# Where a PSUM bank, a lag and sixteen weight tiles go in a two-layer decoder kernel

## The chip, the cores and the metric

The kernel runs on one core of one Trainium2 chip. Its time is the device time of one execution in microseconds (us), median of several runs. TensorE (PE) multiplies matrices from SBUF into PSUM, which has eight banks of 128 x 512 f32 values; VectorE (DVE) and ScalarE (ACT) read PSUM and SBUF; GpSimd (POOL) works on SBUF; SyncE (SP) issues most of the loads.

## The reference

A sequence of 512 tokens of width 1024 goes through two layers. Layer A computes 12 heads of sparse attention in 3 groups of 4 (compressed blocks, selected blocks, sliding window) beside 4 heads of attention to a memory of 256 tokens, then a squared-ReLU MLP with 4096 hidden units. Layer B computes dilated attention with 3 groups of 8 heads over keys and values that are made once from the stream, again with memory attention, and a second MLP. All in float32:

```
for layer in range(2):
    h = rmsnorm(x, attn_norm[layer])
    mem_kv = rmsnorm(mem, mem_norm[layer]) @ w_mem_kv[layer]
    if layer == 0:
        q, kc, vc, ks, vs, kw, vw, q_mem, gl = split(h @ a_w_in)
        o_main = nsa_attention(q, kc, vc, ks, vs, kw, vw, gl, ...)
        w_out = a_w_out
    else:
        k_s, v_s = split(rmsnorm(x, kv_norm) @ w_kv_shared)
        k_shared = rope(rmsnorm(split_heads(k_s, 8), kv_k_norm), pos)
        q, q_mem = split(h @ b_w_in)
        o_main = dilated_attention(q, k_shared, split_heads(v_s, 8), b_q_norm)
        w_out = b_w_out
    o_mem = memory_attention(q_mem, mem_kv, mem_q_norm[layer], mem_k_norm[layer])
    x = x + concat([o_main, o_mem]) @ w_out
    x = x + square(relu(rmsnorm(x, mlp_norm[layer]) @ w_up[layer])) @ w_down[layer]
```

## The kernel before, in words

**Matmuls in three parts.** Float32 operands are split into a rounded high part and a low part, and `mm3` (lines 260 to 262) multiplies high by high, high by low and low by high into one bank. A weight tile is loaded into a staging buffer `st` (three of them) by SP, ScalarE writes its high part (`wsplit`, line 253), and VectorE or GpSimd its low part (line 255): a letter "v" or "g" says which. The string "gv" takes turns. The staging buffer is free when both parts are written, and there are four buffers `w` for the result.

**PSUM.** The eight banks lie in four pools: `pacc` (2) for projections, `pS` (2) for attention scores, `pT` (3) for transposes, `pO` (1) for attention outputs. `ps()` hands out one bank of a pool.

**Attention as items.** An `Item` has a front (scores on PE into `pS`, row maximum on VectorE at lines 1043, 1055 or 713, exponentials on ScalarE at line 216 through `marked`, scaling on GpSimd at line 722) and a back (transposes of the probabilities on PE into `pT`, copies out at line 730 by ScalarE or, in layer A every third time, VectorE, and products with the values into `pO`). `attend` runs the fronts in order and each back a number of items later (`lag`, here 1). After each front and each back, `tick` takes one step from a list `side` and, by a ratio for each segment, steps from a queue of other work `work`: the next group's projection, memory keys, the first part of the output projection. In layer A an item's scores take one bank for the first two query blocks and two for the other two; in layer B one. Layer A's scores are at lines 972 (compressed blocks), 1039 and 1052, its transposes at 996, 1081 and 1087; layer B's scores at 1536, 1540, 1544 and 1550, its transposes at 1584 and 1593.

**Projections.** `proj` multiplies in blocks of 128 tokens, each in one bank, and `evac` reads the bank: `normf` (lines 501 to 515) finds the norms of the heads by a square, a sum and a few small operations, a product with the gain follows, then rotation on GpSimd, and some steps later transposes of the result (`q_out`, lines 755 and 765) into `pT`. The first projection keeps four banks at once, two of them from `pS`. The projection `w_a0` after it takes its four banks as `pS`, `pacc`, `pacc`, `pS`, with low parts on GpSimd.

**Output projections.** `outpart` goes over eight output tiles; it is called twice in each layer, and takes its weights' low parts in turns by GpSimd and VectorE. Its first part is `work` beside the last attention items, its second comes after them. Line 1149 adds the result to the stream.

The build's scheduler orders each engine's instructions ahead of time, by the order of the program and its own model of when things are ready.

Of the kernel before, what the change touches and what calls it, by code (L numbers as in the profile page):

```python
# [11 lines left out]
ALU = mybir.AluOpType  # L12
# [7 lines left out]
HD = 64  # L20
# [13 lines left out]
def bcast(ap, dim, n):  # L34

    a = [list(x) for x in ap.ap]
    a.insert(dim, [0, n])
    return bass.AP(tensor=ap.tensor, offset=ap.offset, ap=a)
# [9 lines left out]
RB = (1.58, 1.85, 1.49, 2.4, 1.9)  # L48
# [20 lines left out]
def drain(*gens):  # L69
    for g in gens:  # L70
        for _ in g:
            pass
# [20 lines left out]
class Work:  # L93


    def __init__(self):
        self.q, self.done = [], set()
# [83 lines left out]
class K:  # L181
    def __init__(self, ctx, tc, ins, out):
        self.tc, self.nc, self.ins, self.out = tc, tc.nc, ins, out
        ps = lambda n, b: ctx.enter_context(tc.tile_pool(name=n, bufs=b, space=bass.MemoryType.PSUM))
        sb = lambda n, b: ctx.enter_context(tc.tile_pool(name=n, bufs=b))
        self.pacc, self.pS, self.pT, self.pO = ps("acc", 2), ps("ps", 2), ps("pt", 3), ps("po", 1)
        self.one = sb("one", 1)
        self.sb = sb("sb", 1)
        self.dram = ctx.enter_context(tc.tile_pool(name="dram", bufs=1, space=bass.MemoryType.DRAM))
        self.n = 0  # L190
        self.ev = 3
        self.staged = []
        self.sums, self.marks = {}, []
        self.adds, self.far = self.blocks(), 5
        self.lab = "s"
# [9 lines left out]

    def ps(self, pool, shape, dt=F32):
        self.n += 1
        return pool.tile(shape, dt, name=f"{self.lab}_{pool.name}_{self.n}", tag=pool.name)

    def c(self, name, shape, dt=F32):  # L210
        return self.one.tile(shape, dt, name=name)
# [288 lines left out]
    def normf(self, raw, nh, e):  # L500

        nc = self.nc
        p = raw.shape[0]
        sq = self.t("sq", [p, nh, HD])
        nc.scalar.activation(sq.rearrange("p h d -> p (h d)"), raw, AF.Square)
        ss = self.t("r4", [p, nh])
        nc.vector.tensor_reduce(out=ss, in_=sq, axis=AX.X, op=ALU.add)
        y = self.t("r5", [p, 3, nh])
        nc.scalar.activation(y[:, 0], ss, AF.Ln, scale=1.0 / HD, bias=e[:, 0:1])
        nc.scalar.activation(y[:, 1], y[:, 0], AF.Exp, scale=-0.5, bias=self.eps[0:p, 2:3])  # L510
        nc.scalar.activation(y[:, 2], y[:, 1], AF.Square)
        f = self.t("r6", [p, nh])
        nc.vector.scalar_tensor_tensor(out=f, in0=ss, scalar=e[:, 1:2], in1=y[:, 2], op0=ALU.add, op1=ALU.mult)
        nc.vector.scalar_tensor_tensor(out=f, in0=f, scalar=-1.5, in1=y[:, 1], op0=ALU.add, op1=ALU.mult)
        return f
# [96 lines left out]
    def mem_q(self, l, xg, wsrc, e, res):  # L612
        nc = self.nc
        q4 = [self.t("qk", [P, 2, S], F32R) for _ in range(2)]
        gq = self.grow(f"mq{l}")

        def evac(b, ps):
            f = self.normf(ps, 4, e[:, b])
            G = self.t("tq", [P, 4, HD])
            nc.vector.tensor_tensor(  # L620
                out=G, in0=ps.rearrange("p (h d) -> p h d", d=HD), in1=bcast(gq[:, 0], 1, 4), op=ALU.mult
            )
            blk = slice(b * P, (b + 1) * P)
            return self.q_out(G, f, [q4[0][:, :, blk], q4[1][:, :, blk]])

        yield from self.proj(xg, wsrc, 256, evac, per=4, lo="gv")
        res.append(q4)

    def mem_keys(self, l, kf, res):
# [485 lines left out]
    def outpart(self, oT, k0, k1, wsrc, xsrc, w0, wide=1):  # L1115


        nc = self.nc
        nk = k1 - k0
        while len(oT) < k1:  # L1120
            yield WAIT
        oT = oT[k0:k1]
        for m0 in range(0, KT, wide):
            ms = range(m0, min(m0 + wide, KT))
            w, ps = {}, {}

            def step(m, k):
                self.mm3(
                    ps[m], [w[m][:, h, k * P : (k + 1) * P] for h in (0, 1)], [oT[k][:, h, :] for h in (0, 1)],
                    k == 0, k == nk - 1,  # L1130
                )

            for m in ms:
                c = slice(w0 * P, (w0 + nk) * P)
                w[m] = self.wload(wsrc[m][:, c], "gv"[m % 2])
                ps[m] = self.ps(self.pacc if xsrc is not None else self.pS, [P, S])
                for k in range(nk - 1):
                    step(m, k)
                    yield
            for m in ms:  # L1140
                step(m, nk - 1)
                yield
                if xsrc is not None:
                    xo = self.t("st", [P, S])
                    nc.sync.dma_start(xo, xsrc[m])
                    self.x[m] = self.t("x", [P, S])
                else:
                    xo = self.x[m]
                nc.vector.tensor_tensor(out=self.x[m], in0=ps[m], in1=xo, op=ALU.add)
# [243 lines left out]
    def layer_b(self):  # L1393
        self.ev = 1000000
        nc, ins = self.nc, self.ins
        self.setup_b()
        st = self.rt
        xk = self.xk
        xd = self.xd
        vd = self.dram.tile([S, 512], F32, name="vd")  # L1400

        def evac_v(b, ps):
            t = self.t("raw", [P, 512])
            nc.scalar.activation(t, ps, AF.Copy, scale=st[0][:, b : b + 1])
            nc.gpsimd.dma_start(vd[b * P : (b + 1) * P, :], t)

        kn = [None] * NB

        gk = self.grow("kk")

        def evac_k(b, ps):
            e = st[1]
            kt = self.t("x", [P, 8, HD])
            kn[b] = kt
            for hf in range(2):
                rw = ps[:, hf * 256 : (hf + 1) * 256]
                f = self.normf(rw, 4, e[:, b])
                kh = kt[:, hf * 4 : hf * 4 + 4]
                nc.vector.tensor_tensor(
                    out=kh, in0=rw.rearrange("p (h d) -> p h d", d=HD), in1=bcast(gk[:, 0], 1, 4), op=ALU.mult  # L1420
                )
                self.rope(kh, self.cs[:, b])
                nc.gpsimd.tensor_tensor(out=kh, in0=kh, in1=bcast(f, 2, HD), op=ALU.mult)

        drain(
            self.proj(xk, ins["w_kv"][0], 512, evac_k, pool=[self.pS, self.pS, self.pacc, self.pacc], order=(2, 3, 0, 1))
        )
        drain(self.proj(xk, ins["w_kv"][1], 512, evac_v, pool=self.pS))
        xg = [self.t("act", [P, 2, S], F32R) for _ in range(KT)]
        for m in range(KT):  # L1430
            for h in range(2):
                self.gained(xg[m], m, h, "attn1")
        e = st[1]
        oT, om, pb, qm, kk = [], [], [[] for _ in range(4)], [], []
        kp, vals = [[] for _ in range(4)], [[] for _ in range(4)]
        work, side, seen = Work(), Work(), []
        for sp in range(1, 4):
            work.add(self.proj_b(sp, xg, e, pb[sp]))
            work.add(self.keys_b(sp, kn, vd, kp[sp]), sp, lambda sp=sp: seen.count(sp - 1) == 8)
        work.add(self.mem_q(1, xg, ins["w_bm"], e, qm))  # L1440
        work.add(self.mem_keys(1, self.kf1, kk), "mem")
        work.add(self.outpart(oT, 0, 3, ins["w_bo"], xd, 0))
        first = weave(self.proj_b(0, xg, e, pb[0], self.pS, DX), self.keys_b(0, kn, vd, kp[0]), WK)
        for i, _ in enumerate(first):
            for _ in range(WB[1] if i >= WB[0] else 0):
                work.step()
        items = []
        for sp in range(4):
            items += self.attn_b(sp, pb[sp], kp[sp], oT, side)
        items += self.mem_items(self.kf1, qm, kk, om, 4, "mem")  # L1450
        attend(items, work, side, RB, seen)
        while side.step() is not END or work.step() is not END:
            pass
        drain(self.outpart(oT + om, 3, 6, ins["w_bo"], None, 3, 3))
# [233 lines left out]
def build(tc, ins, out):  # L1688
    with ExitStack() as ctx:
        k = K(ctx, tc, ins, out)  # L1690
        nc = tc.nc
        k.setup()
        k.layer_a()
        k.mlp(0)
        k.layer_b()
        k.mlp(1)
# [111 lines left out]
```

## Time and profile before

| | us |
|---|---|
| median of 3 runs | 1285.7 |
| lowest and highest | 1283.59, 1286.21 |
| profiled execution, own time | 1285.64 |
| its span, first to last instruction | 1283.9 |
| PE busy | 1243.8 |
| VectorE busy | 829.8 |
| ScalarE busy | 756.1 |
| GpSimd busy | 365.7 |

The stages, in us from the start of the span: layer A's projections and attention 0 to about 335, its MLP to about 690, shared keys and values and layer B's first queries to about 790, layer B's attention to about 907, the end of its memory attention and output projection to about 937, the second MLP to the end. Matmuls overlap in PE, so that busy time is not the same as full rate; the idle time before an instruction, in brackets in the timelines, is time in which PE had nothing in flight. The granted clock is 1.00 at full speed.

### The profile page before, as it was taken

The page shows a single profiled execution, that of the slowest core. Times are in us where ns is not written, and L with a number is a line of the kernel's source. Part 1 is how long each engine was busy: PE and PEld are TensorE (multiplying, and loading weights), DVE is VectorE, ACT ScalarE, POOL GpSimd, SP SyncE. Part 2 cuts the span into 40 slices and gives each one's busy share as a digit, 9 for nine tenths or more (in the row PEclk, how much of TensorE's full clock was granted, in tenths as well). Part 3 has the DMA queues.
Part 4 walks back from the last instruction along what each step waited for, and adds up shares of the span by engine and source line. Part 5 has one row for each costly group of instructions (what it writes and reads, how often), then busy time and mean ns, then how long its engine had stood idle before and what let it go on. Part 6 is the DMA issues. An engine that isn't in the chain of part 4 may idle for free.

```text
span 1283.9 us, 18311 instructions
## 1 busy us (share of the span) xinstructions
PE 1243.8 (97%) x6416; PEld 1024.4 (80%) x6416; DVE 829.8 (65%) x1510; ACT 756.1 (59%) x1684; POOL 365.7 (28%) x470
## 2 busy tenths in 40 slices
PE   8899998899999999999999999999999999999998
PEld 6868877677788888888888899887778888888887
DVE  6746875654565657566579577676757656656566
ACT  6745777774575364453648467778657455354462
POOL 4445774543140000000002778363413000000000
PEclk9899999999999999999999999999999999999999
DMA  7521332334478797797975422110359789697434
GB/s 262 196 91 54 97 100 91 67 75 116 147 240 235 244 267 218 263 239 225 275 210 185 133 85 66 52 46 10 102 167 278 211 275 251 198 295 228 143 105 164
DMA packets 61836, 215.27 MB, mean 168 GB/s; under 512 B 6736, under 2 KB 14928, under 8 KB 61232
## 3 DMA queue, kind: packets, MB, share of 16 engines
q1 hardware_dynamic: 50800, 143.72, 34.0%
q0 software_dynamic: 9344, 35.77, 14.2%
q10 hardware_dynamic: 1600, 34.61, 7.5%
q8 instruction: 51, 0.84, 0.3%
q14 instruction: 41, 0.34, 0.1%
HBM read 208.83 MB, written 72.35 MB: 219 GB/s over the span
## 4 chain that ended last, share of the span: by engine, by line
PE 78%; DVE 8%; ACT 6%; DMA 4%; issue 2%; POOL 1%; SPq 0%; ACTq 0%; POOLq 0%; DVEq 0%
PE s_ps L260 13%; PE s_ps L261 13%; PE s_ps L262 13%; PE s_acc L260 6%; PE s_acc L261 5%; PE s_acc L262 5%; PE s_pt L260 3%; PE s_pt L261 3%; PE s_pt L262 3%; PE s_po L734 3%; ACT s_p L216 2%; DVE s_w L255 1%; PE s_ps L1052 1%; DMA s_st<-in_w_ao_dram 1%; DVE s_act L277 1%
## 5 line engine op out<-in xcount | busy, mean ns | idle before, releaser
L255 DVE TENSOR_TENSOR s_w<-s_st,s_w 128x1024 fp32r<-128x1024 f32 (+3 forms) x236 | 279.0, 1187 | 253.3 <-ACT s_w L253 252.6
L253 ACT ACTIVATE s_w<-s_st 128x1024 fp32r<-128x1024 f32 (+4 forms) x260 | 251.3, 970 | 191.1 <-DMA s_st<-sum 40.0
L260 PE MATMUL s_ps<-s_act,s_w 128*128 128x512 f32 x568 | 222.8, 394 | 2.0 <-ACT s_act L295 1.4
L261 PE MATMUL s_ps<-s_act,s_w 128*128 128x512 f32 x568 | 221.5, 391 | 0.0
L262 PE MATMUL s_ps<-s_act,s_w 128*128 128x512 f32 x568 | 221.2, 390 | 0.0
L260 PEld LDWEIGHTS s_ps<-s_act,s_w 128*128 128x128 f32 x568 | 106.4, 188 | 26.3 <-ACT s_act L295 3.2
L262 PEld LDWEIGHTS s_ps<-s_act,s_w 128*128 128x128 f32 x568 | 106.7, 188 | 22.4
L261 PEld LDWEIGHTS s_ps<-s_act,s_w 128*128 128x128 f32 x568 | 106.7, 188 | 22.2 <-DVE s_act L298 0.9
L216 ACT ACTIVATE s_p<-s_ps 128x512 f32<-128x512 f32 x64 | 38.3, 598 | 121.6 <-PE s_ps L262 120.7
L260 PE MATMUL s_acc<-s_w,s_act 128*128 128x512 f32 (+3 forms) x288 | 102.5, 362 | 4.9 <-DVE s_r L497 3.4
L261 PE MATMUL s_acc<-s_w,s_act 128*128 128x512 f32 (+3 forms) x288 | 102.6, 357 | 1.6 <-POOL s_w L255 1.5
L262 PE MATMUL s_acc<-s_w,s_act 128*128 128x512 f32 (+3 forms) x288 | 100.8, 355 | 0.0
L1170 POOL DMA_DIRECT2D sum<-in_w_db_dram x16 | 14.4, 899 | 288.8 <-ACT s_p L216 287.1
L216 ACT ACTIVATE s_p<-s_ps,s_nm 128x256 f32<-128x256 f32 (+3 forms) x128 | 65.0, 515 | 22.3 <-DVE s_nm L1055 10.2
L722 POOL TENSOR_SCALAR s_p<-s_p,s_cr,s_ab 128x128 f32<-128x128 f32 (+3 forms) x96 | 59.0, 638 | 47.5 <-DVE s_cr L1063 45.9
L260 PEld LDWEIGHTS s_acc<-s_w,s_act 128*128 128x128 f32 x288 | 55.0, 192 | 10.6 <-ACT s_x L942 3.4
L730 ACT ACTIVATE s_pt<-s_pt 128x512 f32<-128x512 f32 (+2 forms) x101 | 51.9, 523 | 15.9 <-PE s_pt L1087 5.3
L261 PEld LDWEIGHTS s_acc<-s_w,s_act 128*128 128x128 f32 x288 | 55.2, 192 | 6.4 <-POOL s_w L255 1.7
L295 ACT ACTIVATE s_qk<-s_p 128x256 fp32r<-128x256 f32 (+1 forms) x96 | 46.9, 488 | 21.0 <-DVE s_p L1180 19.1
L262 PEld LDWEIGHTS s_acc<-s_w,s_act 128*128 128x128 f32 x288 | 55.2, 192 | 4.2 <-issue 0.2
L1170 POOL DMA_DIRECT2D sum<-sum x16 | 14.1, 883 | 151.3 <-DMA sum<-sum 64.6
L298 DVE TENSOR_TENSOR s_qk<-s_p,s_qk 128x256 fp32r<-128x256 f32 (+1 forms) x96 | 50.1, 522 | 0.7 <-ACT s_qk L295 0.6
(329 smaller groups left out, 2913.9 us busy)
## 6 DMA issues: line engine op xcount, KB each, us to landing
s_st<-in_w_up_dram SPq DMA_DIRECT2D x64, 512.0 KB, 4.2
s_st<-sum SPq DMA_DIRECT2D x64, 512.0 KB, 7.3
s_st<-in_w_db_dram SPq DMA_DIRECT2D x48, 512.0 KB, 4.6
sum<-in_w_db_dram POOLq DMA_DIRECT2D x16, 1024.0 KB, 14.4
sum<-sum POOLq DMA_DIRECT2D x16, 1024.0 KB, 12.1
s_st<-in_w_bq_dram SPq DMA_DIRECT2D x16, 384.0 KB, 3.4
s_st<-in_w_ag_dram SPq DMA_DIRECT2D x11, 512.0 KB, 3.6
s_w<-in_w_c_dram SPq DMA_DIRECT2D x8, 512.0 KB, 4.5
```

The lines of the kernel that those rows point to most:

```text
L216: return lambda *a, **k: self.marks.append(f(*a, **k))
L253: nc.scalar.activation(w[:, 0], st, AF.Copy)
L255: e.tensor_tensor(out=w[:, 1], in0=st, in1=w[:, 0], op=ALU.subtract)
L260: mm(ps, lh[0], rh[0], start=start, stop=False, skip_group_check=again)
L261: mm(ps, lh[0], rh[1], start=False, stop=False, skip_group_check=again)
L262: mm(ps, lh[1], rh[0], start=False, stop=stop, skip_group_check=again)
L295: nc.scalar.activation(dst[:, 0], src, AF.Copy)
L298: nc.vector.tensor_tensor(out=dst[:, 1], in0=src, in1=dst[:, 0], op=ALU.subtract)
L722: self.nc.gpsimd.tensor_scalar(out=p, in0=p, scalar1=c, scalar2=g, op0=ALU.mult, op1=ALU.mult)
L730: self.turned = self.nc.scalar.activation(dst, src, AF.Copy)
L734: i = self.nc.tensor.matmul(*a, **k)
L1170: self.behind(self.nc.gpsimd.dma_start(t[o], x, accum_op=ALU.add, max_dma_last_dim=4096))
```

## The change

Five edits. (1) The third transpose bank becomes a pool `px` of its own, and `ps()` gives every third request of one chosen pool to it: of `pS` through layer A, of `pT` from the first MLP on. So layer A has three score banks and two transpose banks, and the rest two and three. (2) `attend` in layer B runs with a lag of 2. (3) `outpart` and `mem_q` (both layers) take the low parts of all their weights on VectorE. (4) The shared keys' norms are found over 8 heads of a block at once, and the product with the gain is one instruction; rotation and scaling stay in halves of 4 heads. (5) `normf` puts its squares into the buffers `p2` (six) where there are over 6 heads, and in `sq` (one) otherwise.

```diff
-        self.pacc, self.pS, self.pT, self.pO = ps("acc", 2), ps("ps", 2), ps("pt", 3), ps("po", 1)
+        self.pacc, self.pS, self.pT, self.pO = ps("acc", 2), ps("ps", 2), ps("pt", 2), ps("po", 1)
+        self.px, self.third, self.turns = ps("px", 1), self.pS, 0
...
     def ps(self, pool, shape, dt=F32):
         self.n += 1
-        return pool.tile(shape, dt, name=f"{self.lab}_{pool.name}_{self.n}", tag=pool.name)
+        name = f"{self.lab}_{pool.name}_{self.n}"
+        if pool is self.third:
+            self.turns += 1
+            if self.turns % 3 == 0:
+                pool = self.px
+        return pool.tile(shape, dt, name=name, tag=pool.name)
+
+    def third_to(self, pool):
+
+        self.third, self.turns = pool, 0
...
-        sq = self.t("sq", [p, nh, HD])
+        sq = self.t("p2" if nh > 6 else "sq", [p, nh, HD])
...
-        yield from self.proj(xg, wsrc, 256, evac, per=4, lo="gv")
+        yield from self.proj(xg, wsrc, 256, evac, per=4, lo="v")
...
-                w[m] = self.wload(wsrc[m][:, c], "gv"[m % 2])
+                w[m] = self.wload(wsrc[m][:, c], "v")
...
+            f = self.normf(ps, 8, e[:, b])
+            nc.vector.tensor_tensor(
+                out=kt, in0=ps.rearrange("p (h d) -> p h d", d=HD), in1=bcast(gk[:, 0], 1, 8), op=ALU.mult
+            )
             for hf in range(2):
-                rw = ps[:, hf * 256 : (hf + 1) * 256]
-                f = self.normf(rw, 4, e[:, b])
                 kh = kt[:, hf * 4 : hf * 4 + 4]
-                nc.vector.tensor_tensor(
-                    out=kh, in0=rw.rearrange("p (h d) -> p h d", d=HD), in1=bcast(gk[:, 0], 1, 4), op=ALU.mult
-                )
                 self.rope(kh, self.cs[:, b])
-                nc.gpsimd.tensor_tensor(out=kh, in0=kh, in1=bcast(f, 2, HD), op=ALU.mult)
+                nc.gpsimd.tensor_tensor(out=kh, in0=kh, in1=bcast(f[:, hf * 4 : hf * 4 + 4], 2, HD), op=ALU.mult)
...
-        attend(items, work, side, RB, seen)
+        attend(items, work, side, RB, seen, 2)
...
         k.layer_a()
+        k.third_to(k.pT)
         k.mlp(0)
```

## The prediction

> **What bounds the kernel now.** I read the busy line first, then a table by stage, then what TensorE (PE) waits for in the two attention stages, then single places in order of time. From the page, and from the table of windows (columns: stage, its length, then busy us and count for PE, weight loads, VectorE, ScalarE, GpSimd, then granted clock, DMA share, GB/s):
>
> ```profile
> PE 1243.8 (97%) x6416; PEld 1024.4 (80%) x6416; DVE 829.8 (65%) x1510; ACT 756.1 (59%) x1684; POOL 365.7 (28%) x470
> 0.00:335.00 335.00, 312.63 (x1792) 245.42 (x1792) 207.29 (x498) 213.35 (x608) 169.82 (x249) 0.97 0.37 115
> 335.00:690.00 355.00, 354.92 (x1596) 294.08 (x1597) 229.95 (x336) 194.84 (x297) 28.26 (x26) 1.00 0.81 239
> 690.00:790.00 100.00, 95.76 (x517) 86.25 (x515) 73.09 (x144) 61.85 (x173) 73.38 (x90) 0.98 0.33 103
> 790.00:907.00 117.00, 109.30 (x841) 95.64 (x840) 81.61 (x180) 89.29 (x296) 54.97 (x63) 1.00 0.14 41
> 907.00:937.00 30.00, 28.39 (x148) 19.55 (x147) 20.50 (x47) 19.26 (x56) 15.16 (x22) 1.00 0.33 100
> 937.00:1284.00 347.00, 342.85 (x1531) 283.46 (x1529) 217.36 (x311) 177.51 (x259) 24.09 (x21) 1.00 0.71 213
> ```
>
> PE is the bound: of a span of 1283.9 us it is busy 1243.8. The MLP of layer A (335 to 690) leaves 0.08 us idle, and that of layer B gives up 4 us of which the change touches nothing; so 702 us are out of reach, either way: there the third transpose bank is the same rotation of three under another name. What can move is idle time of layer A (22.4 us), of layer B's projections (4.2), its attention (7.7) and its end (1.6), 36 us together, and time at a lower clock. The waits of PE in those stages, layer A from 40 us on, then layer B:
>
> ```profile
> PE s_ps L1052 <- ACT s_p L216: 6.0, 11, 1.2
> PE s_ps L1039 <- ACT s_p L216: 3.9, 8, 1.4
> ...
> PE s_pt L1087 <- POOL s_p L722: 1.6, 3, 0.7
> PE s_pt L1081 <- ACT s_pt L730: 0.6, 1, 0.6
> ...
> PE s_pt L1584 <- ACT s_p L216: 3.5, 5, 1.4
> PE s_acc L261 <- POOL s_w L255: 1.5, 1, 1.5
> ```
>
> In layer A the scores (L1039, L1052) wait 9.9 us for exponentials, that is for one of two score banks to be read out, while the transposes wait 0.6 us for a transpose bank (s_pt released by the copy L730). In layer B the transposes (L1584) wait for exponentials.
>
> **The change part by part.** I sum against the profiled execution's own 1285.64 us; the median of the runs is 1285.7, so nothing is lost between them. The build fixes each engine's order in advance, and the order after the change is not in this trace: every term has a wide interval for that.
>
> *The bank, first use: the end of the first projection.* Four banks hold group 0's projection; the next projection (420 columns) asks for a bank of the score pool first and, having none, waits until the first is read out. With a third bank it starts at once. PE and GpSimd in order of time:
>
> ```profile
> 29.05 0.98 PE L489 MATMUL s_pt<-on,s_p 128*128 128x1 f32 x8
> 33.41 0.51 PE L260 MATMUL s_acc<-s_w,s_act 128*128 128x420 f32 x1 [3.39 <-DVE s_r L497]
> 34.07 0.55 PE L262 MATMUL s_acc<-s_w,s_act 128*128 128x420 f32 x1
> 34.42 0.55 PE L260 MATMUL s_acc<-s_w,s_act 128*128 128x420 f32 x1
> 38.10 0.35 PE L261 MATMUL s_acc<-s_w,s_act 128*128 128x420 f32 x1
> 38.29 0.35 PE L262 MATMUL s_acc<-s_w,s_act 128*128 128x420 f32 x1
> ...
> 28.88 1.96 POOL L255 TENSOR_TENSOR s_w<-s_st,s_w 128x840 fp32r<-128x840 f32 x1
> 33.54 2.17 POOL L255 TENSOR_TENSOR s_w<-s_st,s_w 128x840 fp32r<-128x840 f32 x1 [2.71 <-ACT s_w L253]
> ```
>
> PE stands 3.39 us, then issues at 0.35 us a matmul in place of 0.19 for about ten matmuls, 1.6 us more: 5.0 in all. The third weight slab is complete at 30.84 (28.88 + 1.96), so 18 matmuls of the first block could run from 30.0 to 33.4; the fourth is complete only at 35.71. If PE's order then waits for it, only about 2.7 us come back (18 matmuls done at 35.71, where now (35.71 - 33.41)/0.35 = 6.6 are done: 11.4 x 0.19 = 2.2, and 0.5 of slow clock); if the next block is drawn ahead, 5.0. I take 3.5; ends 0 and 5.0.
>
> *The bank in layer A's attention.* It is ScalarE that reads the score banks, and where PE waits longest it has little to spare. Here is a window before and one after the clock fell, three times, and two windows in layer B:
>
> ```profile
> 57.50:60.90 3.40, 1.95 (x11) 1.23 (x9) 2.67 (x7) 3.30 (x13) 0.68 (x2) 1.00 1.01 400
> 60.90:67.70 6.80, 6.10 (x23) 5.06 (x22) 4.35 (x10) 5.84 (x18) 6.80 (x17) 0.50 0.38 154
> 207.70:211.10 3.40, 2.08 (x11) 1.10 (x9) 2.57 (x8) 3.37 (x11) 1.80 (x4) 1.00 0.02 5
> 211.10:214.50 3.40, 3.27 (x18) 2.14 (x20) 1.08 (x4) 1.74 (x9) 2.70 (x6) 0.50 0.94 292
> 241.80:245.20 3.40, 1.75 (x8) 1.13 (x8) 2.54 (x9) 3.11 (x12) 0.92 (x2) 1.00 0.00 0
> 245.20:248.60 3.40, 3.03 (x10) 2.64 (x11) 2.33 (x9) 1.87 (x7) 3.22 (x7) 0.51 0.00 0
> 842.58:846.00 3.42, 1.88 (x15) 1.73 (x15) 3.42 (x4) 2.27 (x7) 3.42 (x3) 1.00 0.45 116
> 883.53:886.94 3.41, 2.03 (x19) 1.81 (x19) 1.52 (x7) 2.31 (x11) 0.00 (x0) 1.00 0.02 5
> ```
>
> ScalarE is busy 3.30, 3.37 and 3.11 us of 3.40: a bank more lets PE run ahead by one score group, but exponentials come no faster there. Elsewhere they do catch up. So of 9.9 us I take 4.0, the shorter waits. Each fall of the clock to 0.50 follows a window in which PE was busy some 2 us of 3.4, and costs half its length: 3.4 + 1.7 + 1.7 = 6.8 us. I take back one short one, 1.7. Against this stands the transposes' bank, three to two. 24 of the attention's 48 items in layer A move two transpose tiles, and each is copied out in
>
> ```profile
> L730 ACT ACTIVATE s_pt<-s_pt 128x512 f32<-128x512 f32 x50 | 29.6, 600 | 3.2 <-PE s_pt L1087 1.5 <-PE s_pt L755 0.4 <-PE s_pt L676 0.4
> ```
>
> 0.6 us: if each pair must wait for one copy, 24 x 0.6 = 14.4 us; if items stay some 4 us apart as now, nothing. I take 2.0, near the low end, since with three banks the wait is only 0.6. Net -3.7; ends -16.7 (9.9 and 6.8, no cost) and +14.4.
>
> The Trainium skill, "TensorE: Matmul & The Clock Gate", section "What's actually happening", states that the half clock comes after at least one idle window of about 3.4 us. By that rule no clock returns with waits of about 1 us, and the sum would be 1.7 us higher. The rows differ: 1.75 to 2.08 us of PE in a window of 3.4 were enough, though 1.88 and 2.03 in layer B were not; the rows decide, and I count one case.
>
> *Low parts by VectorE.* Nine weight tiles of each layer (four of the eight output-weight tiles in each of two passes, and one of the memory query) leave GpSimd's queue, where they stand among the softmax scalings:
>
> ```profile
> L255 POOL TENSOR_TENSOR s_w<-s_st,s_w 128x512 fp32r<-128x512 f32 x8 | 10.3, 1285 | 19.8 <-ACT s_w L253 19.8
> L255 DVE TENSOR_TENSOR s_w<-s_st,s_w 128x512 fp32r<-128x512 f32 x16 | 12.8, 817 | 8.1 <-ACT s_w L253 8.1
> L255 POOL TENSOR_TENSOR s_w<-s_st,s_w 128x384 fp32r<-128x384 f32 x8 | 8.1, 1019 | 19.0 <-ACT s_w L253 19.0
> L255 DVE TENSOR_TENSOR s_w<-s_st,s_w 128x384 fp32r<-128x384 f32 x8 | 5.8, 729 | 1.5 <-ACT s_w L253 1.5
> 840.96 3.39 POOL L255 TENSOR_TENSOR s_w<-s_st,s_w 128x1024 fp32r<-128x1024 f32 x1
> 842.39 2.11 DVE L698 TENSOR_TENSOR s_ki<-s_x,s_ki 128x128 fp32r<-128x128 f32 x1
> ...
> 300.93 1.24 POOL s_w L255
> 302.19 3.57 DMA s_st<-in_w_ao_dram
> ```
>
> A tile is ready 0.47 us (512 columns) or 0.29 us (384) sooner, frees its staging buffer as much sooner, and so lets SP issue the next load sooner; no transfer is added, and no queue but GpSimd's and VectorE's changes. The gain on PE is the 1.5 us wait named for this line, and a share of layer A's tail, where the chain of waits (last two rows) goes from GpSimd's low part to the load that waited for its buffer; I take 2.0 together. Price: VectorE does 8 x 0.82 + 8 x 0.73 + two of 1024 columns at about 1.2 = 15 us more in stages where it is busy 62 to 70%. Each waits for ScalarE's high part, and behind it in VectorE's queue stand the row maxima, for which the exponentials wait. Ends: -4 and +3 (a fifth of the 15).
>
> The rows at 841 and 842 us weigh a rule: VectorE's small subtraction of 842.39 ended (844.50) just after GpSimd's low part did (844.35). The Trainium skill, "SBUF — State Buffer", section "Who interferes with whom", states that a VectorE instruction with two SBUF inputs and a GpSimd one that reads SBUF exclude each other. The trace agrees. By that rule the 15 us now hold up GpSimd's scalings instead, while the 18.4 us of the sixteen GpSimd tiles above no longer hold up VectorE; so the sum stays.
>
> *Shared keys' norms over 8 heads.* Four blocks each lose one set of small operations, by
>
> ```profile
> L507 DVE TENSOR_REDUCE s_r<-s_sq 128x4 f32<-128x256 f32 x20 | 8.2, 411 | 4.4 <-ACT s_sq L505 4.4
> L510 ACT ACTIVATE s_r<-s_r,eps 128x4 f32<-128x4 f32 x20 | 6.0, 302 | 0.3
> ```
>
> three ScalarE operations of about 0.3 us each (3.6 us in all) and some 2 us of VectorE, while squares, sums and products keep their elements. All four blocks have banks of their own, so PE has the other blocks' matmuls as cover. I take 0.5; ends -2 and +1 (the first half's rotation now starts after all eight heads' product).
>
> *Layer B's second halves two items later.* With two score banks, item i's scores cannot start before item i-2's exponentials are done; so transposes of i-2 put behind them find their data, and the five waits (3.5 us) go. Next late is the bank itself: the scores still wait, as in layer A. I take 1.5. A probability tile lives one item longer: three of six buffers, as many as fit. Price: attention's outputs come one item later, (907 - 790)/32 = 3.7 us, and the output projection's first part, which fills the last items, starts later by that; it has more slots than steps, so I take nothing. Ends -3.5 and +3.7.
>
> Sum: -3.5 - 3.7 - 2.0 - 0.5 - 1.5 = -11.2, so 1285.6 - 11.2 = 1274.4 us.
>
> **Rivals.** (1) *Two transpose banks bind layer A*, and the score bank brings nothing: 1285.6 - 7.5 (the other four terms) + 7.2 to 14.4 = 1285 to 1292.5, middle 1289. It is slower by over 0.2% once PE waits over 10.1 us more in front of transposes. For it: 96 softmax halves and the projections' query transposes share these banks, all copied by ScalarE, which is full in the windows above. Against it: 0.6 us now. (2) *The waits only move*: ScalarE sets the pace, so bank, lag and norms bring nothing; only 1.5 of the low parts and a little of the first wait are left: 1283 to 1285. (3) *All of it and the clock*: 5.0 + 9.9 + 6.8 - 2.0 + 2.0 + 0.5 + 1.5 = 23.7: 1262.
>
> **How the numbers follow.** The forecast (1268 to 1282, its terms at half and at one and a half) gets 0.60, rival 1 0.13, rival 2 0.17, rival 3 0.10. About 0.2% (2.6 us) is what can be told from no change. Faster by more: 0.60 + 0.10 + 0.03 of rival 2 = 0.73; within: 0.14; slower: 0.13. For 8 in 10 the range keeps the forecast, rival 2's better part and half of rival 3: 1264 to 1286.
>
> **What would show it.** Right: the 3.39 us gap after 29 us is filled; L1039 and L1052 wait under 6 us for L216; L1081 and L1087 wait under 3 us more for copies; no PE wait for L255 on GpSimd in layer B; L1584's waits under 1 us. Wrong: transposes of layer A waiting for L730 by over 8 us; a new wait of PE on row maxima (VectorE); the end of layer B later against its attention.

## The result and the profile after

The changed kernel takes 1274.6 us (median of 4 runs, 1274.44 to 1277.08), the kernel before 1285.95 (4 runs, 1283.59 to 1287.45): a ratio of 0.9912, 95% interval 0.9892 to 0.9932. The forecast was 1274.4. As the experiments show, the sum came out right with several terms wrong. Single runs that took far longer than the rest of their kernel (1394 us and more) are left out of the medians and ratios below.

The page's busy line of the changed kernel (its profiled execution took 1274.7 us):

```profile
PE 1238.3 (97%) x6416; PEld 1019.0 (80%) x6416; DVE 829.8 (65%) x1512; ACT 753.0 (59%) x1668; POOL 348.3 (27%) x452
```

Its stages, as before (stage, length, busy us and counts of PE, weight loads, VectorE, ScalarE, GpSimd, then clock, DMA share, GB/s):

```profile
0.00:335.00 335.00, 316.48 (x1832) 247.21 (x1833) 216.08 (x514) 216.23 (x614) 163.91 (x242) 1.00 0.39 118
690.00:790.00 100.00, 95.50 (x541) 86.60 (x541) 66.91 (x113) 59.55 (x165) 80.58 (x101) 1.00 0.28 86
790.00:907.00 117.00, 111.53 (x849) 97.64 (x846) 85.98 (x204) 91.03 (x300) 49.39 (x59) 1.00 0.18 52
907.00:937.00 30.00, 27.99 (x125) 18.89 (x124) 20.54 (x34) 16.51 (x34) 5.12 (x7) 0.94 0.42 127
```

Span and mean granted clock, of the changed kernel and then of the one before:

```profile
core 0: 1272.9 us, clock 0.998
```
```profile
core 0: 1283.9 us, clock 0.992
```

PE's work is the same 6416 matmuls, yet it is busy 5.5 us less: at half clock the 420-column matmuls of the prediction's rows follow each other after 0.35 us in place of 0.19, and the half clock is nearly gone. With clocks of 1 and 0.5 alone, (1 - mean clock) x span is the most that half clock can have cost: (1 - 0.992) x 1283.9 = 10 us before, (1 - 0.998) x 1272.9 = 2.5 us after. So at most some 8 of the 11 us between these two profiles are clock. PE's busy and idle time share the 11 us in halves: it is busy 5.5 us less, and its idle time falls by 5.5 us too (40.1 to 34.6). That the clock rises is not one profile's luck: over all runs its mean is 0.990 for the kernel before (65 runs, in the sessions of the experiments below) and 0.998 for the changed one (4 runs).

What PE waits for in the changed kernel, layer A from 40 us on (its first lines), then layer B; the lines of the code have moved by 9 or 10, so L1062 and L1049 are the scores that were L1052 and L1039, L226 the exponentials, L740 the copies out:

```profile
PE s_ps L1062 <- ACT s_p L226: 3.5, 9, 1.0
PE s_acc L270 <- DVE s_tq L957: 1.5, 1, 1.5
PE s_po L744 <- ACT s_pt L740: 1.2, 1, 1.2
PE s_pt L775 <- ACT s_qk L715: 1.1, 2, 0.9
PE s_ps L667 <- ACT s_p L226: 1.1, 1, 1.1
PE s_pt L765 <- DVE s_qki L708: 1.0, 1, 1.0
PE s_pt L1006 <- ACT s_pt L740: 0.8, 1, 0.8
...
PE s_pt L1097 <- ACT s_pt L740: 0.5, 2, 0.3
...
PE s_ps L1049 <- ACT s_p L226: 0.3, 2, 0.2
...
PE s_ps L271 <- DVE s_act L1692: 1.7, 1, 1.7
PE s_ps L1553 <- ACT s_p L226: 1.3, 3, 0.8
PE s_ps L1545 <- ACT s_p L226: 0.9, 2, 0.7
```

In layer A the self-attention scores wait 3.8 us for exponentials where they waited 9.9. Other waits came in their place: transposes wait for copies, about 2.4 us for a bank (L775, L1006, L1097), the memory's scores (L667) 1.1 us where they waited 0.2, and 2.5 us are for VectorE (L957, L708). In layer B no transpose (L1593) waits for exponentials any more; the scores wait 2.2 us for their bank in its place. The first projection's end, PE in order of time:

```profile
28.91 0.35 PE L270 MATMUL s_ps<-s_w,s_act 128*128 128x420 f32 x1
31.39 0.95 PE L499 MATMUL s_pt<-on,s_p 128*128 128x1 f32 x8
33.82 0.43 PE L270 MATMUL s_acc<-s_w,s_act 128*128 128x420 f32 x1 [0.42 <-DVE s_tq L957]
```

The 420-column projection starts at 28.91 in place of 33.41, ahead even of the memory's statistics (L499), at 0.19 us a matmul, and PE's gap of 3.39 us is gone. Where the two traces part, by the starts of the same PE instructions in the timelines:

| start of | before | changed | difference | step |
|---|---|---|---|---|
| first score of layer A | 54.91 | 51.04 | -3.87 | -3.87 |
| last self-attention score of layer A (L1052) | 285.60 | 275.03 | -10.57 | -6.70 |
| first MLP's norm's sums (L489) | 377.18 | 368.15 | -9.03 | +1.54 |
| first score of layer B (L1536) | 759.87 | 751.11 | -8.76 | +0.27 |
| last dilated score of layer B (L1544) | 893.86 | 881.08 | -12.78 | -4.02 |
| second MLP's norm's sums (L489) | 974.02 | 963.16 | -10.86 | +1.92 |

Not all marks stand behind equal work. At the third, the fifth and the sixth as many matmuls have started in both kernels, at the first and the fourth six small transposes fewer in the changed one; but at the second it has done 34 fewer, transposes and products of a back that come after that score. So the second and the third step are to be read together: -5.16.

A step of 1.5 us is near what one program repeats: the kernel below that changes layer B alone, with PE's order in layer A unchanged, reached the third mark 1.5 us early. It can be more: the kernel below with the first gap filled, whose PE order from the third mark to the sixth is that of before, took 5.3 us longer between them, with 20.5 us at half clock in place of 3.4 (summed from the trace's clock records, as are all such sums below).

### The profile page after: what moved, and what is told of

Read it like the earlier page. It is cut to its first block, busy times and chain, and to the rows that moved or that the text cites. A ratio compares the mean times of both kernels' runs of the same rounds, so it can differ in the third digit from the quotient of the medians.

```text
span 1272.9 us, 18280 instructions
## 1 busy us (share of the span) xinstructions
PE 1238.3 (97%) x6416; PEld 1019.0 (80%) x6416; DVE 829.8 (65%) x1512; ACT 753.0 (59%) x1668; POOL 348.3 (27%) x452
## 3 DMA queue, kind: packets, MB, share of 16 engines
q0 software_dynamic: 9344, 35.77, 14.2%
## 4 chain that ended last, share of the span: by engine, by line
PE 78%; DVE 8%; ACT 7%; POOL 2%; DMA 2%; issue 2%; ACTq 0%; POOLq 0%; DVEq 0%
PE s_ps L270 13%; PE s_ps L271 13%; PE s_ps L272 13%; PE s_acc L270 6%; PE s_acc L271 6%; PE s_acc L272 6%; PE s_po L744 3%; PE s_pt L271 3%; PE s_pt L270 3%; PE s_pt L272 3%; ACT s_p L226 2%; DVE s_w L265 1%; PE s_acc L877 1%; PE s_acc L576 1%; DVE s_act L287 1%
## 5 line engine op out<-in xcount | busy, mean ns | idle before, releaser
L265 DVE TENSOR_TENSOR s_w<-s_st,s_w 128x1024 fp32r<-128x1024 f32 (+3 forms) x254 | 290.3, 1150 | 260.7 <-ACT s_w L263 250.8
L226 ACT ACTIVATE s_p<-s_ps 128x512 f32<-128x512 f32 x64 | 38.2, 598 | 117.9 <-PE s_ps L272 117.1
L270 PE MATMUL s_acc<-s_w,s_act 128*128 128x512 f32 (+3 forms) x288 | 100.9, 356 | 5.4 <-DVE s_tq L1477 2.5
L271 PE MATMUL s_acc<-s_w,s_act 128*128 128x512 f32 (+3 forms) x288 | 101.0, 352 | 0.0
L272 PE MATMUL s_acc<-s_w,s_act 128*128 128x512 f32 (+3 forms) x288 | 99.8, 351 | 0.0
L732 POOL TENSOR_SCALAR s_p<-s_p,s_cr,s_ab 128x128 f32<-128x128 f32 (+3 forms) x96 | 61.9, 681 | 53.6 <-DVE s_cr L1073 26.4
L226 ACT ACTIVATE s_p<-s_ps,s_nm 128x256 f32<-128x256 f32 (+3 forms) x128 | 65.5, 523 | 12.2 <-DVE s_nm L723 2.9
L740 ACT ACTIVATE s_pt<-s_pt 128x512 f32<-128x512 f32 (+2 forms) x101 | 52.8, 526 | 20.0 <-PE s_pt L1097 7.5
L270 PEld LDWEIGHTS s_acc<-s_w,s_act 128*128 128x128 f32 x288 | 54.0, 188 | 12.2 <-DVE s_tq L1477 2.9
L271 PEld LDWEIGHTS s_acc<-s_w,s_act 128*128 128x128 f32 x288 | 54.3, 189 | 4.6 <-issue 0.4
L272 PEld LDWEIGHTS s_acc<-s_w,s_act 128*128 128x128 f32 x288 | 54.2, 188 | 4.6 <-issue 0.2
```

Of the source, the lines that this page charges most:

```text
L226: return lambda *a, **k: self.marks.append(f(*a, **k))
L265: e.tensor_tensor(out=w[:, 1], in0=st, in1=w[:, 0], op=ALU.subtract)
L270: mm(ps, lh[0], rh[0], start=start, stop=False, skip_group_check=again)
L271: mm(ps, lh[0], rh[1], start=False, stop=False, skip_group_check=again)
L272: mm(ps, lh[1], rh[0], start=False, stop=stop, skip_group_check=again)
L732: self.nc.gpsimd.tensor_scalar(out=p, in0=p, scalar1=c, scalar2=g, op0=ALU.mult, op1=ALU.mult)
```

## The experiments

Two theories stood at first: that the edits' gains add, in the sizes of the prediction; and that they add in the sizes of the steps above. Four kernels each undo one edit of the changed kernel. Each ratio is to the kernel before in the same session, with its 95% interval; times are medians.

**Without the bank.** `ps("pt", 3)`, and `ps()`, `third_to` and their call as before.

```diff
-        self.pacc, self.pS, self.pT, self.pO = ps("acc", 2), ps("ps", 2), ps("pt", 2), ps("po", 1)
-        self.px, self.third, self.turns = ps("px", 1), self.pS, 0
+        self.pacc, self.pS, self.pT, self.pO = ps("acc", 2), ps("ps", 2), ps("pt", 3), ps("po", 1)
...
-        k.third_to(k.pT)
```

> The changed kernel with two score banks and three transpose banks throughout, everything else as changed. Theory one (the prediction's terms): the bank is worth 3.5 + 3.7 = 7.2 us, so about 1281.8 us. Theory two (places where the two traces part): the bank is worth 3.9 us before the first scores and 6.7 us in layer A's attention, 10.6 in all, so about 1285, with the 3.4 us gap of TensorE after 29 us back. Rival (the parts only move waits and the low parts do the work): within 2 us of the changed kernel.

1292.3 us, 1.0053 (1.0033 to 1.0074): 17.7 us slower than the changed kernel, and slower than before. Neither theory had that: the other edits together, without the bank, are a loss. Its waits in layer A:

```profile
PE s_ps L1039 <- ACT s_p L216: 5.6, 8, 1.4
PE s_ps L1052 <- ACT s_p L216: 5.5, 11, 1.2
PE s_ps L260 <- ACT s_p L216: 2.7, 1, 2.7
```

Scores wait 11.1 us, and the output projection's second pass (L260, which asks for a score bank) waits 2.7 us for the last memory scores. Layer A ends 5.4 us later than before.

**Without the lag.** Layer B's second halves one item later.

```diff
-        attend(items, work, side, RB, seen, 2)
+        attend(items, work, side, RB, seen)
```

> The changed kernel with layer B's second halves one item later again. Theory one: 1.5 us slower, about 1276. Theory two: the lag gains 4 us within layer B's attention and gives 3 back at its end, where TensorE waits 1.7 us for the last normalised output and the clock falls; so about 1275.5, the last transposes of layer B's attention 4 us later than in the changed kernel, and no wait of the output projection for that output at the end. Rival (the lag is free of cost at the end): 4 us slower, about 1278.6, with the wait at the end still there.

1280.4 us, 0.9970 (0.9955 to 0.9985): the lag is worth 5.8 us here, four times the prediction's term and more than theory two's. At the last dilated score this kernel is 4.1 us behind the changed one, but 1.6 of that stands already at layer B's first score. The loss at the end is not the lag's: this kernel loses more there, 4.8 us against 1.9. The single wait of 1.7 us for L1692 is gone, as theory two said, but others stand in its place, the longest 2.0 us (L744 for L1683).

**Without the move of the low parts.**

```diff
-        yield from self.proj(xg, wsrc, 256, evac, per=4, lo="v")
+        yield from self.proj(xg, wsrc, 256, evac, per=4, lo="gv")
...
-                w[m] = self.wload(wsrc[m][:, c], "v")
+                w[m] = self.wload(wsrc[m][:, c], "gv"[m % 2])
```

> The changed kernel with the low parts of the output and memory query weights by GpSimd and VectorE in turns again. Theory one: 2.0 us slower, about 1276.6. Theory two: layer A's end, where the two traces lose 1.5 us between the last scores and the second layer's statistics, is better with GpSimd's help, layer B's memory query worse by up to 1.5 us; within 1 us of the changed kernel. Rival (VectorE's 15 us more are on the path): 1 to 3 us faster than the changed kernel.

1279.0 us, 0.9944 (0.9924 to 0.9964): the move is worth 4.4 us, more than either theory had. Where theory two expected a loss, at layer A's end, the move gains 1.9 us: from the last self-attention score to the first MLP's norm this kernel takes 94.8 us, and the changed kernel and the four others here that share its PE order in layer A take 92.8 to 93.1. Where the rest lies its profile doesn't tell, which has 10.2 us at half clock in layer B.

**Without the wider norms.** `evac_k` and the buffer of `normf` as before.

```diff
-            f = self.normf(ps, 8, e[:, b])
...
+                f = self.normf(rw, 4, e[:, b])
```

> The changed kernel with the shared keys' norms in two halves of 4 heads again. Theory one: 0.5 us slower, about 1275.1. Theory two: nothing, since the two traces keep their distance between the first MLP's end and layer B's first scores. Rival (eight heads at once hold the rotation back): up to 1 us faster.

1273.6 us, 0.9902 (0.9882 to 0.9921): 1 us faster than the changed kernel, with intervals that overlap; on that edit the sign was probably wrong, and it is small.

The four undone edits make 17.7 + 5.8 + 4.4 - 1.1 = 26.8 us, against 11.3 for all. The terms don't add, so single edits were put into the kernel before.

**The bank alone.** To the kernel before:

```diff
+        self.px, self.third, self.turns = ps("px", 1), self.pS, 0
...
+        k.third_to(k.pT)
```

> The kernel before with the bank's edit alone. Theory one (terms add): 7.2 us faster than before by the prediction, or up to 17.7 by what the changed kernel lost without it. Theory two (the edits depend on each other: without the bank, low parts by VectorE cost layer A some 5 us, with it they gain some 3): the bank alone gives what the changed kernel without the other edits keeps, about 5 to 6 us, with layer A's end 5 us earlier, as where only the low parts were undone.

1284.9 us, 1.0000 (0.9987 to 1.0013): nothing. In the profile layer A does end 4.8 us earlier, as theory two said, but layer B gives 5 us back.

**The low parts alone.** To the kernel before:

```diff
+        yield from self.proj(xg, wsrc, 256, evac, per=4, lo="v")
...
+                w[m] = self.wload(wsrc[m][:, c], "v")
```

> The kernel before with the low parts of the output and memory query weights by VectorE alone. Theory one (terms add): 2.0 us faster by the prediction, 4.4 by the kernel in which they were undone. Theory two (they depend on the bank): layer A's end about 5 us later, layer B's attention up to 5 us earlier, in all 0 to 5 us slower than before.

1294.2 us, 1.0069 (1.0041 to 1.0097): 9 us slower, more than any theory had. The two edits need each other. The same square stands with the lag in all four kernels: 1280.0 us with neither (the lag alone, told below), 1279.0 with the bank, 1292.3 with the low parts, 1274.6 with both; the wider norms, which the first of these lacks, are worth about 1 us. Layer A shows how. There the kernels have only four orders of PE's work, and each order has two profiles or more. Up to the first MLP's norm, in us:

| layer A's program | kernels | time | PE idle | of it behind the last self-attention score | at half clock |
|---|---|---|---|---|---|
| neither | before, lag alone | 375.7 to 377.2 | 22.0 to 22.5 | 2.4 to 2.6 | 13.7 to 17.1 |
| bank | bank alone, low parts undone | 371.7 to 372.4 | 20.7 to 21.4 | 3.0 to 3.2 | 3.4 |
| low parts | low parts alone, bank undone | 380.7 to 382.5 | 26.4 to 27.6 | 5.0 to 5.5 | 13.7 to 17.1 |
| both | changed kernel, four others | 367.7 to 369.7 | 18.3 to 19.0 | 1.7 to 2.0 | 0 to 3.4 |

The bank takes away 10 us of half clock or more in either company. The low parts add 4 to 6 us of idle time without the bank, and take away 2 to 3 with it. The chain of waits between 275 and 335 us (shares of it by engine and line; the answer cuts the row short), in the kernel before, with the bank alone, then in the changed kernel:

```profile
by line: DMA s_st<-in_w_ao_dram 23.0%; issue 10.2%; PE s_po L734 6.4%; ACT s_p L216 5.7%; PE s_acc L262 4.7%; PE s_acc L260 4.7%; PE s_acc L261 4.2%; DVE s_w L255 3.8%; POOL s_p L722 3.6%; PE s_ps L260 3.5%; DVE s_x L1149 3.3%; PE s_ps L261
```
```profile
by line: DMA s_st<-in_w_ao_dram 36.8%; ACT s_w L263 7.3%; POOL s_w L265 6.5%; PE s_ps L270 5.8%; PE s_po L744 5.7%; PE s_ps L272 4.6%; PE s_ps L271 4.3%; DVE s_w L265 3.9%; issue 3.6%; PE s_ps L667 3.6%; PE s_pt L1097 3.4%; PE s_acc L272 2.
```
```profile
by line: PE s_po L744 14.0%; PE s_acc L270 12.6%; PE s_acc L271 12.3%; PE s_acc L272 12.3%; PE s_ps L270 8.4%; PE s_ps L272 7.7%; PE s_ps L271 7.7%; PE s_ps L667 6.8%; PE s_pt L686 5.8%; PE s_pt L1097 4.8%; PE s_po L1012 1.8%; ACT s_act L30
```

The output weights' loads hold 23.0% of the chain before. With the bank alone they hold 36.8%, and GpSimd's low parts (L265) 6.5%: that staging buffers come free too late there is likely, since a load waits for its buffer. With both edits that chain is gone from the row, and PE's matmuls stand in it. The other way round, with the low parts alone, the loads still hold 28.9%, and the kernel's waits in layer A are:

```profile
PE s_ps L1052 <- ACT s_p L216: 6.7, 11, 1.5
PE s_ps L1039 <- ACT s_p L216: 5.2, 8, 1.4
PE s_ps L260 <- ACT s_p L216: 2.5, 1, 2.5
```

The scores' wait is 11.9 us, and the second pass's 2.5 us appears as it did without the bank; it is about what the low parts add behind the last score. That VectorE's low parts stand ahead of row maxima there, while two banks still hold the scores back, is likely, not shown. In layer B the low parts alone lose 5 us more, in a profile with 13.7 us at half clock from 823 us on. The kernel with the first gap filled has such a stretch from 816 us on, with PE's order in layer B as before, so these 5 us can be chance.

**The bank for the first projection only.** Behind the weaving of the first projection with `w_a0`, every third request goes to the transposes again.

```diff
+        self.third_to(self.pT)
```

> The changed kernel, but the bank goes back to the transposes right after the projection w_a0, ahead of layer A's attention. Theory one: keeps 3.5 of the bank's 7.2, so 3.7 us slower than the changed kernel, about 1278.3. Theory two: keeps 4 us and loses all that the bank does in layer A's attention, about 13 of 17.7 us, so about 1288; TensorE's waits of scores for exponentials in layer A back to 10 us and the clock falls there again. Rival (the first use alone does it, by an earlier start and another clock phase): within 2 us of the changed kernel.

1287.0 us, 1.0005 (0.9990 to 1.0019): 12.4 us slower than the changed kernel. The first gap alone brings nothing of the whole. But this kernel loses two things in layer A's attention: the third score bank, and the free choice among three transpose banks, which the turn alone (below) shows to cost. How the 12.4 us divide between them is not shown. Waits in layer A (this kernel's lines are one further):

```profile
PE s_ps L1063 <- ACT s_p L226: 5.6, 8, 1.8
PE s_ps L1050 <- ACT s_p L226: 3.3, 6, 1.3
PE s_ps L270 <- ACT s_p L226: 2.4, 2, 1.2
```

8.9 us of score waits are back, and the clock falls twice in layer A.

**The lag alone.** To the kernel before:

```diff
+        attend(items, work, side, RB, seen, 2)
```

> The kernel before with the lag of two items alone: the corner that is missing of the eight with and without bank, low parts and lag. If the terms added, 5.8 us faster than before, as much as the changed kernel lost without the lag; by the prediction 1.5 faster. Theory of dependence (the lag pays where layer B's score waits are short and low parts come early): between 3 us faster and no change. Layer A is the same program as before in all cases.

1280.0 us, 0.9944 (0.9923 to 0.9965): 5.9 us faster than before, as much as the lag is worth in the changed kernel. The lag adds; it needs nothing else. PE's idle time says so too: between the two MLPs' norms it falls by 3.3 us here (13.6 to 10.3) and by 3.5 in the changed kernel (15.6 without the lag, 12.0 with it).

**The turn alone.** Two score banks throughout, and the third transpose bank as a pool of its own that takes every third transpose request.

```diff
+        self.px, self.third, self.turns = ps("px", 1), self.pT, 0
```

> The kernel before with its third transpose bank named apart and every third transpose request bound to it, through the whole program; score banks two, everything else as before. It tests whether the bound turn itself costs layer B what the kernel with the bank alone lost there. Theory one (the same rotation under another name, as the prediction has it): within 1 us of before. Theory two (a request bound to one bank waits though another is free): layer B 3 to 5 us longer, layer A too.

1301.7 us, 1.0100 (1.0071 to 1.0129). The prediction took this rotation for the same as before, at nothing; it costs 13 to 16 us. Layer A ends 13.5 us later, with 5.5 us more of idle time and 10 us more at half clock, and layer B loses 4; the first MLP, from its norm on, keeps its time to 0.1 us, so there the prediction holds. How it costs is not settled: a request may wait for its one bank though another is free, and the build's order changes too (of PE's instructions in layer A's attention, some 40% no longer stand in the order of before). The runs don't separate the two. It says what the bank's edit contains in layer B, where it does nothing but bind the turn. The bank alone lost 5 us there, and from the first MLP's norm to the second its order of PE's work is the same as here. Both lose 4.1 us behind the last dilated score, with 4.5 us idle there where the kernel before has 2.4, and with a fall of the clock.

**The end of layer B by both engines, and norms in halves.** The changed kernel with two edits: `"gv"` in the last pass of layer B's output projection alone, and the norms as before.

```diff
-        drain(self.outpart(oT + om, 3, 6, ins["w_bo"], None, 3, 3))
+        drain(self.outpart(oT + om, 3, 6, ins["w_bo"], None, 3, 3, "gv"))
```

> The changed kernel with the shared keys' norms in halves again, and GpSimd taking turns with VectorE for the low parts in the second pass of layer B's output projection alone. Theory two: 1 us from the norms, and up to 2 us of the 3 that the changed kernel loses between layer B's last scores and its end, about 1271.5. Rival (that loss comes from the lag, not from VectorE's load): 1273.5, as with the norms alone.

1272.7 us, 0.9901 (0.9882 to 0.9919): the lowest median, 1.9 us under the changed kernel and 0.8 under the kernel with the norms alone undone, inside the intervals. It loses nothing between the last dilated scores and the second MLP's norm, where the changed kernel lost 1.9. But the kernel with the norms alone undone, whose order of PE's work is the same, loses only 0.3 there, and so does the kernel with the bank for the first projection only, whose order there is the changed kernel's: most of the 1.9 is a fall of the clock that these two don't have. The wait for the last normalised output (1.5 us there) is gone here, so a share of GpSimd may be worth about 1 us at this end; the medians don't show it.

**The third bank with the scores in layer B too.** The kernel just told of, with the bank handed over twice more.

```diff
+        k.third_to(k.pS)
         k.layer_b()
+        k.third_to(k.pT)
         k.mlp(1)
```

> The changed kernel with norms in halves and GpSimd's turns in the last pass (1272.7 us), and the third bank with the scores in layer B's projections and attention too, with the transposes only in the two MLPs. Theory one (layer B's scores wait for banks as layer A's did): 2 to 4 us faster, 1269 to 1271, the 2.2 us of score waits there gone. Rival (with the lag of two the scores run ahead far enough, and two transpose banks cost more): 0 to 5 us slower.

1285.0 us, 0.9987 (0.9974 to 1.0001): the rival, and beyond it: 12.3 us slower than that kernel. In layer B PE waits for

```profile
PE s_pt L1509 <- ACT s_qk L1486: 2.6, 2, 2.2
PE s_pt L765 <- DVE s_qki L708: 2.2, 1, 2.2
PE s_pt L1603 <- ACT s_pt L740: 0.7, 2, 0.5
```

keys' transposes that wait for queries' copies out of a bank (L1509), queries' transposes that wait for VectorE's low parts (L765), and transposes that wait for a copy (L1603). From layer B's first score to the last dilated one PE is idle 11.7 us, where the kernel with two score banks is idle 6.8. As far as these waits tell, in layer B the scarce banks are the transposes'; the edit also binds the scores' requests by turn and changes the build's order.

**The first gap filled.** The kernel before, with 12 matmuls that nothing reads in the gap at 30 us.

```diff
+        spare = self.ps(self.pT, [P, S])
+        for _ in range(12):
+            nc.tensor.matmul(spare, xg[7][:, 0, 0:P], xg[7][:, 0, :], start=True, stop=True)
```

> The kernel before with 12 matmuls of 128 x 512 that nothing reads, put behind the first projection, in the 3.4 us in which TensorE waits for the first bank. The wait itself stays: the projection w_a0 starts at 33.4 us as before. Theory one (the clock falls because that window is idle, and costs half the time that follows): no half clock after it, matmuls at 0.19 us from the start, and the projection's end 1.6 us earlier. Rival (the slow start has another reason, weights that are late): end unchanged. The whole time 1 to 2 us less, or within noise.

PE in order of time:

```profile
29.98 3.02 PE L815 MATMUL s_pt<-s_act 128*128 128x512 f32 x12
33.33 0.43 PE L260 MATMUL s_acc<-s_w,s_act 128*128 128x420 f32 x1 [0.33 <-DVE s_r L497]
33.60 0.35 PE L261 MATMUL s_acc<-s_w,s_act 128*128 128x420 f32 x1
33.79 0.36 PE L262 MATMUL s_acc<-s_w,s_act 128*128 128x420 f32 x1
33.98 0.35 PE L260 MATMUL s_acc<-s_w,s_act 128*128 128x420 f32 x1
```

The wait is the same (33.33 for 33.41), the matmuls come at 0.19 us at once, and the projection ends 0.96 us earlier, less than the 1.6 foreseen. 1283.3 us, 0.9971 (0.9955 to 0.9987). So idleness, not the weights, makes the slow start, and filling the gap with work that nobody reads cost nothing there. How much of the 0.3% in the whole is its doing is not shown: with the extra bank the build's order in the rest of layer A is another. The Trainium skill, "TensorE: Matmul & The Clock Gate", section "What's actually happening", puts the half clock down to an idle window of some 3.4 us; here the trace agrees: before the fall at 33.62 us PE had been busy 0.2 us of 3.41.

## Why the prediction was right, and where it wasn't

*First use of the bank.* Right: 3.9 us by the first score, for 3.5.

*The bank in layer A's attention.* The direction was right, the size too small, and its make-up wrong: the waits brought less than was set, the clock more. From the first score to the last self-attention score, the row of the changed kernel, then that of before:

```profile
51.04:275.31 224.27, 210.09 (x1278) 162.54 (x1277) 144.91 (x367) 151.78 (x456) 128.35 (x194) 1.00 0.33 96
```
```profile
54.91:285.93 231.02, 215.87 (x1308) 168.92 (x1307) 148.01 (x370) 153.88 (x459) 128.91 (x196) 0.97 0.32 94
```

The self-attention scores' waits fell by 6.1 us, where 4.0 were set, but PE's idle time fell only from 15.2 to 14.2: other waits took most of it back. So of the net 2.0 us of waits that were set (4.0 less 2.0 for the two transpose banks) about 1.0 came. One clock fall was to go, at 1.7 us; all three went, 13.7 us at half clock, up to 6.8 us of time. This repeats: up to the first MLP's norm the seven profiles with the third score bank through layer A have 0 or 3.4 us at half clock, the seven without it 6.8 to 27.3. By the rule of the Trainium skill weighed there ("TensorE: Matmul & The Clock Gate", section "What's actually happening"), no clock would have come back; the measurement decides against it, since no score wait was longer than 1.4 us before. Why PE no longer falls to half clock, though it is idle nearly as long, the runs don't show; that its idle time is spread more evenly is a guess.

Rival 1 did not come: its 8 us of copies are 2.4 (and not ScalarE alone copies, as it says: in layer A VectorE makes every third copy of probabilities). Rival 2, that the waits only move, is nearly what happened to PE's idle time in this stage; what it left out is the clock.

*The same rotation under another name.* This failed. It was priced at nothing in words that looked at the MLPs alone, where it is true; for layer B's projections and attention, where every third transpose request is bound too, the prediction has no term. The turn alone costs 13 to 16 us. Most of that lies in layer A, where the changed kernel binds scores and not transposes; in layer B it is 4 to 5 us with a lag of one. What it costs with the changed kernel's lag of two no run separates.

*Low parts by VectorE.* 2.0 us were set; 4.4 in the changed kernel, and a loss of 9 alone. The step that failed is the sum itself, which gives an edit one worth in all company. Of its ends, -4 was about reached and +3 passed by far, one in each company. The chain that it named (GpSimd's low part, then the load) is on the path and goes with both edits; but the loads hold the chain before as well, and the low parts alone leave them there.

*Norms.* 0.5 us set, about -1 measured, near the noise.

*The lag.* Mechanism right (the five waits are gone, and in the changed kernel the score bank is next late), size wrong: 5.8 us for 1.5, the low end of -3.5 passed. PE's idle time fell by 3.3 to 3.5 us, so in sum as much as the five waits was won, not 1.5 us of it; with the lag alone a clock fall of 3.4 us in layer B went as well, for which the prediction had no term there. The rest, 1 to 2 us, stays open; the build orders PE's work in layer B anew. The end of layer B came later against its attention, one of the signs of being wrong (1.7 us for L1692 and a clock of 0.73 right after):

```profile
915.00:920.00 5.00, 3.30 (x9) 1.84 (x10) 2.58 (x4) 1.74 (x4) 0.00 (x0) 0.73 0.40 122
```

But it is not a price of the lag: without the lag the end takes 2.8 us longer still. The wait for L1692 is there only in kernels that have the lag, the low parts and the bank's turn together, and a share of GpSimd takes it away.

So the sum agreed because misses of both signs met: more from lag, low parts and clock, less from layer A's waits and from a turn that was not priced. That it lay within 0.2 us is chance.

## What to carry to other kernels

When PE is at 97% and the rest is many short waits, price each edit in the company of the others: here the bank alone gained nothing, the low parts alone lost 9 us, and both with the lag and the norms gained 11. Count the clock as a term of its own, at most (1 - mean clock) x span, and look for windows in which PE is busy only half the time. Compare two traces at marks behind equal work, and read idle time and half clock apart: a wait that goes may come back in another line. And a buffer pool that is split, with requests bound in turn, is not the same as one pool of the same size.

## What was not expected of the hardware

The same program repeats only to about 0.8%, and the clock goes with it: among the runs of the kernel before, 1281.3 us had a mean clock of 0.994 and 1291.75 us one of 0.983; 0.011 of the span is 14 us, the difference 10.5. In the profile of the kernel before, every half-clock stretch that ends inside it lasts 3.41 us or twice that, and each begins a whole multiple of 3.41 us after the clock first rose at 6.32 us (at 33.62, 60.93, 211.12, 245.25 and 774.31); in the other profiles too such stretches last whole multiples. So it matters how a sparse stretch of PE lies on that grid. The kernel before and the one with the first gap filled, with one order of PE's work from the first MLP's norm to the second's, took 596.8 and 602.1 us for it, with 3.4 and 20.5 us at half clock. Single profiles of one kernel differ by that much.
